# Softmax sums of an attention kernel: broadcast through DRAM in place of a TensorE transpose, halves added on GpSimd

## The chip, the cores and the metric

The kernel runs on one NeuronCore of a Trainium2 chip. The metric is the device time of one execution in microseconds (us). Before the change it is 2939.41 us, the median of three runs (2938.95 to 2943.35).

## What is computed

A backbone of two layers over 1024 latent tokens and 256 context tokens, width 1024: a Conformer convolution layer, then a grouped-query attention layer, each followed by a dense SwiGLU FFN. The change lies in the attention:

```python
def gqa_sdpa(q, k, v):
    B, Q, H, Dh = q.shape                      # 16 heads of 64, 4 key heads
    qg = q.reshape(B, Q, N_KV_HEADS, KV_GROUP, Dh)
    s = jnp.einsum("bqkgd,bskd->bkgqs", qg, k).astype(jnp.float32) * (Dh ** -0.5)
    p = jax.nn.softmax(s, axis=-1).astype(v.dtype)
    o = jnp.einsum("bkgqs,bskd->bqkgd", p, v)
    return o.reshape(B, Q, H * Dh)
```

In the second layer only the latent tokens ask: 1024 queries against 1280 keys.

## The kernel before

Everything is in fp32, and a product in full precision is built of fp32r products of high and low parts. The attention is cut into 32 units: one unit is one key head `t` with its 4 query heads and 128 queries (`attn_stream`). The scores of a unit (`scores`, L1116) are 24 matmuls, which fill two PSUM regions of 128x1280 in turn. VectorE scales a region into SBUF and takes its minimum (L1122), ScalarE does the exponential with the row sum as a side result (L1124). Then `values` works on the unit, while the scores of the next unit run: for each of 10 key tiles, TensorE transposes the probabilities of four heads (L1134), ScalarE rounds the tile to its high part (L1137), VectorE subtracts it for the low part (L1138), and two matmuls with the values add to the accumulator `av` (L1140 high, L1141 low). The `av` accumulator is one PSUM bank (bank 7), so the next unit's first L1140 waits until the last reader of this unit has left it.

`av` holds, for each half of its 128 rows, a product with the high and one with the low part of the values. The end of a unit adds the halves (ScalarE copies one, L1151; VectorE adds the other, L1152), and divides by the softmax sums. The sums lie with the queries on partitions and are needed with the queries along the free axis: GpSimd repeats the reciprocals (L1147), TensorE transposes them into the same bank 7 (L1155), and VectorE multiplies (L1156). The result goes to DRAM (`od`, issued by GpSimd, L1450); the last unit of a half stays in SBUF (`olast`).

Units 0 to 15 (the first 512 queries) run first. During units 0 and 1, projections of the layer run beside them; units 2 to 15 have the engines to themselves (called the attention stage here, 1641.6 to 1848 us). Units 16 to 31 run beside the output projection and the FFN of the first half (1848 to about 2395 us; 1995 to 2350 is called the FFN stage). The order of each engine's queue is made when the kernel is built, by a scheduler that takes the program's order, priorities (`later`) and its own estimate of durations. GpSimd's queue also issues the loads of queries (`load_q`, L1102: two slots, so a load waits until the unit before has finished its scores) and of keys (`load_k`, L1095: two buffers for units 0 to 15, one afterwards). SBUF scratch `sb` is a ring of four tiles.

Of the kernel before, what the change touches and what calls it, by code (L numbers as in the profile page):

```python
# [8 lines left out]
F32 = mybir.dt.float32  # L9
# [3 lines left out]
ALU = mybir.AluOpType  # L13
AX = mybir.AxisListType

P = 128
# [4 lines left out]
TOK = CTX + SEQ  # L21
# [3 lines left out]
NH, NKV, HD = 16, 4, 64  # L25
# [30 lines left out]
class Kern:  # L56
# [1071 lines left out]
    def values(self, t, Ps, sums, dst, done):  # L1128
        nc, c = self.nc, self.c
        av = self.bank("av")  # L1130
        for j in range(NJ):
            tp = self.bank("pt")
            for h in range(4):
                nc.tensor.transpose(tp[:, h * P:(h + 1) * P], Ps[h][:, j * P:(j + 1) * P], c["ident"])  # L1134
            ph, pl = self.ptring[self.ptslot % len(self.ptring)]
            self.ptslot += 1
            nc.scalar.copy(ph, tp)  # L1137
            nc.vector.tensor_tensor(pl, tp, ph.bitcast(F32), op=ALU.subtract)  # L1138
            with self.later(self.lav):
                nc.tensor.matmul(av, lhsT=self.value(t, j), rhs=ph, start=j == 0, stop=False)  # L1140
                nc.tensor.matmul(av, lhsT=self.value(t, j), rhs=pl, start=False, stop=j == NJ - 1)  # L1141
            yield 0.87

        r = sums[:, 1, :]
        nc.vector.reciprocal(r, sums[:, 0, :])
        rx = self.sb(256)
        nc.gpsimd.tensor_copy(rx.rearrange("p (h d) -> p h d", d=HD), r.unsqueeze(2).to_broadcast([P, 4, HD]))  # L1147
        tmp = self.sb(256).rearrange("p (a q) -> p a q", q=P)
        v = av.rearrange("p (a b q) -> p a b q", b=2, q=P)
        for b, r, o in ((0, slice(0, 64), slice(64, 128)), (1, slice(64, 128), slice(0, 64))):  # L1150
            nc.scalar.copy(tmp[r], v[o, :, b, :])  # L1151
            nc.vector.tensor_tensor(dst[r], v[r, :, b, :], tmp[r], op=ALU.add)  # L1152
        rb = self.bank("av")
        for a in range(2):
            nc.tensor.transpose(rb[:, a * P:(a + 1) * P], rx[:, a * P:(a + 1) * P], c["ident"])  # L1155
        nc.vector.tensor_tensor(dst, dst, rb[:, 0:256].rearrange("p (a q) -> p a q", q=P), op=ALU.mult)  # L1156
        done()
        yield 0.1

# [270 lines left out]
    def attention(self, final, qr):  # L1430
        nc, a, c = self.nc, self.a, self.c
        kbuf = self.T("T3", [P, 2 * TOK], F32R)
        pr1 = self.T("T1", [P, 3, TOK])
        prh = self.T("HS", [P, 4, TOK])
        ptt = self.T("T2", [P, 4, 2, 512], F32R)
        self.ptring = [(ptt[:, i, 0], ptt[:, i, 1]) for i in range(4)]
# [6 lines left out]
        def dst(q0):  # L1443
            def of(t, q):
                if (t, q % 4) == (NKV - 1, 3):
                    return self.olast, lambda: None
                st = self.sb(256).rearrange("p (a q) -> p a q", q=P)

                def done():
                    nc.gpsimd.dma_start(self.od[:, 2 * t:2 * t + 2, q * P:(q + 1) * P], st)  # L1450
                return st, done
            return of
# [11 lines left out]
        pr4 = None  # L1464
        for us in self.attn_stream(units, (self.kub, kbuf), dst(0), True):
            if self.bgq:
                self.pump(self.rate * us)
            elif pr4 is None:
                pr4 = self.T("T5", [P, 3, TOK])
                self.pring = self.pring[:4] + [pr4[:, 0], pr4[:, 1], pr4[:, 2]] + self.pring[4:]  # L1470
                self.set_banks(**alone)
                self.sring = [0, TOK]
# [78 lines left out]
        yacc, n = self.acc(CTX), CTX  # L1551
# [172 lines left out]
```

## Time and profile before

| | |
|---|---|
| median of 3 runs | 2939.41 us |
| the profiled execution | 2938.98 us |
| its span, first to last instruction | 2937.2 us |
| TensorE matmul / weight load busy | 97% / 83% of the span |
| VectorE, ScalarE, GpSimd busy | 74%, 45%, 8% |
| share of TensorE in the chain that ended last | 86% |

The busy share of TensorE is modelled from pipelined matmuls, so it says that the engine had something in flight, not that it worked at its peak. The shares are means over stages that differ; the section on rows has them by stage.

### The profile page before, as it was taken

How to read it: one execution, taken by the hardware profiler on the slowest of the kernel's cores; microseconds unless marked ns; L12 is line 12 of the kernel's file. 1: busy time of each engine (PE TensorE's matmuls, PEld its weight loads, DVE VectorE, ACT ScalarE, POOL GpSimd, SP SyncE). 2: the span in 40 equal slices, each digit the busy share in tenths (PEclk: the TensorE clock that was granted, in tenths of full speed). 3: DMA queues.
4: the chain of work that ended last, by engine and by line, in shares of the span. 5: the costliest groups of instructions: out<-in, count | busy, mean ns of one | idle time of the engine just before them, and what ended most of it. 6: DMA issues, size and time to landing. Idle time of an engine off the chain costs nothing.

```text
span 2937.2 us, 42731 instructions
## 1 busy us (share of the span) xinstructions
PE 2847.7 (97%) x16462; PEld 2446.1 (83%) x16462; DVE 2160.7 (74%) x3746; ACT 1335.5 (45%) x2229; POOL 222.6 (8%) x377
## 2 busy tenths in 40 slices
PE   7999989999999999999999999989999999999998
PEld 6888877888888889989888787767777778889997
DVE  6887788847556378877786899786666666786777
ACT  5222255532222245544445688645555543444444
POOL 0000001011022001000011111110000000010000
PEclk9999999999999999999999999999999999999999
DMA  6443444334356224333345211322222143353332
GB/s 249 140 120 98 116 131 145 135 116 143 115 175 198 65 74 165 114 104 112 109 156 170 88 46 46 97 87 81 66 73 83 60 149 99 110 170 104 102 98 75
DMA packets 131755, 336.58 MB, mean 115 GB/s; under 512 B 31328, under 2 KB 52864, under 8 KB 130656
## 3 DMA queue, kind: packets, MB, share of 16 engines
q1 hardware_dynamic: 78016, 222.33, 24.1%
q0 software_dynamic: 29344, 103.83, 10.7%
q10 hardware_dynamic: 24192, 7.70, 1.1%
q8 instruction: 129, 2.11, 0.3%
q14 instruction: 74, 0.61, 0.1%
HBM read 289.50 MB, written 38.93 MB: 112 GB/s over the span
## 4 chain that ended last, share of the span: by engine, by line
PE 86%; DVE 7%; ACT 2%; issue 2%; DMA 2%; ACTq 0%; POOL 0%; SPq 0%; DVEq 0%; POOLq 0%
PE ps L172 15%; PE ps L173 15%; PE ps L174 15%; PE ps L875 4%; PE ps L877 4%; PE ps L876 4%; PE ps L1116 4%; PE ps L1134 4%; PE ps L1140 2%; PE ps L454 2%; PE ps L455 2%; PE ps L456 2%; PE ps L1141 2%; PE ps L185 1%; PE ps L183 1%
## 5 line engine op out<-in xcount | busy, mean ns | idle before, releaser
L172 PE MATMUL ps<-T,wh 128*128 128x512 f32 (+1 forms) x1360 | 502.5, 370 | 1.4 <-ACT T L161 0.8
L174 PE MATMUL ps<-T,wl 128*128 128x512 f32 (+1 forms) x1360 | 500.4, 368 | 2.0 <-DVE wl L148 2.0
L173 PE MATMUL ps<-T,wh 128*128 128x512 f32 (+1 forms) x1312 | 481.4, 367 | 0.2 <-DVE T L164 0.2
L144 ACT CAST wh<-wr 128x1024 fp32r<-128x1024 f32 (+1 forms) x217 | 225.0, 1037 | 419.9 <-PE ps L173 307.2
L148 DVE TENSOR_TENSOR wl<-wr,wh 128x1024 fp32r<-128x1024 f32 (+1 forms) x217 | 261.9, 1207 | 168.5 <-ACT wh L144 167.1
L875 PE MATMUL ps<-T,wh 128*128 128x256 f32 x1092 | 310.7, 285 | 5.0 <-ACT wh L161 4.5
L876 PE MATMUL ps<-T,wh 128*128 128x256 f32 x1092 | 306.5, 281 | 0.0
L877 PE MATMUL ps<-T,wl 128*128 128x256 f32 x1092 | 305.4, 281 | 0.2 <-DVE wl L164 0.2
L1138 DVE TENSOR_TENSOR T<-ps,T 128x512 fp32r<-128x512 f32 x320 | 216.8, 687 | 107.6 <-ACT T L1137 106.8
L172 PEld LDWEIGHTS ps<-T,wh 128*128 128x128 f32 x1360 | 257.8, 190 | 43.7 <-ACT T L1506 1.7
L174 PEld LDWEIGHTS ps<-T,wl 128*128 128x128 f32 x1360 | 257.7, 190 | 42.4 <-DVE wl L148 2.2
L173 PEld LDWEIGHTS ps<-T,wh 128*128 128x128 f32 x1312 | 248.5, 189 | 38.2 <-DVE T L164 1.3
L1137 ACT CAST T<-ps 128x512 fp32r<-128x512 f32 x320 | 186.0, 586 | 191.1 <-PE ps L1134 177.6
L173 PE MATMUL ps<-HS,wh 128*128 128x512 f32 x656 | 257.9, 393 | 0.0
L172 PE MATMUL ps<-HS,wh 128*128 128x512 f32 x608 | 238.4, 392 | 0.9 <-ACT wh L144 0.9
L174 PE MATMUL ps<-HS,wl 128*128 128x512 f32 x608 | 237.5, 391 | 0.0
L875 PEld LDWEIGHTS ps<-T,wh 128*128 128x128 f32 x1092 | 206.1, 189 | 11.2 <-ACT wh L161 6.7
L876 PEld LDWEIGHTS ps<-T,wh 128*128 128x128 f32 x1092 | 206.6, 189 | 0.5
L877 PEld LDWEIGHTS ps<-T,wl 128*128 128x128 f32 x1092 | 206.2, 189 | 0.6 <-DVE wl L164 0.4
L1134 PE MATMUL ps<-cst,T 128*128 128x128 f32 x1100 | 189.6, 275 | 3.2 <-DVE T L1138 3.1
L1122 DVE TENSOR_SCALAR_CACHE_REDUCE T<-ps,rq 128x1280 f32<-128x1280 f32 x110 | 170.0, 1546 | 27.9 <-PE ps L1116 22.1
L1134 PEld LDWEIGHTS ps<-cst,T 128*128 128x128 f32 x1100 | 132.6, 141 | 49.5 <-DVE T L1138 30.8
(377 smaller groups left out, 6195.9 us busy)
## 6 DMA issues: line engine op xcount, KB each, us to landing
wr<-in_w SPq DMA_DIRECT2D x170, 512.0 KB, 3.6
wr<-in_pw SPq DMA_DIRECT2D x35, 512.0 KB, 3.5
HV<-in_wmodT POOLq DMA_DIRECT2D x56, 256.0 KB, 4.1
q<-in_wmodT POOLq DMA_DIRECT2D x56, 256.0 KB, 3.9
KB<-in_w SPq DMA_DIRECT2D x24, 512.0 KB, 3.6
HR<-in_w SPq DMA_DIRECT2D x23, 512.0 KB, 3.7
q<-in_w SPq DMA_DIRECT2D x23, 512.0 KB, 4.2
q<-qsd POOLq DMA_DIRECT2D x32, 256.0 KB, 3.3
```

The source lines that it names most:

```text
L144: nc.scalar.copy(hi, raw)
L148: nc.vector.tensor_tensor(lo, raw, hi.bitcast(F32), op=ALU.subtract)
L172: nc.tensor.matmul(out[:, :n], lhsT=wh, rhs=xh, start=k == 0, stop=False)
L173: nc.tensor.matmul(out[:, :n], lhsT=wh, rhs=xl, start=False, stop=False)
L174: nc.tensor.matmul(out[:, :n], lhsT=wl, rhs=xh, start=False, stop=k == nk - 1)
L875: nc.tensor.matmul(out, lhsT=wh, rhs=bh, start=first and k == 0, stop=False, **skip)
L876: nc.tensor.matmul(out, lhsT=wh, rhs=bl, start=False, stop=False, **skip)
L877: nc.tensor.matmul(out, lhsT=wl, rhs=bh, start=False, stop=k == 3, **skip)
L1122: nc.vector.tensor_scalar(out=pt, in0=sc, scalar1=rq[:, h:h + 1], scalar2=None, op0=ALU.mult, op1=ALU.min, accum_out=mn)
L1134: nc.tensor.transpose(tp[:, h * P:(h + 1) * P], Ps[h][:, j * P:(j + 1) * P], c["ident"])
L1137: nc.scalar.copy(ph, tp)
L1138: nc.vector.tensor_tensor(pl, tp, ph.bitcast(F32), op=ALU.subtract)
```

## The change

The reciprocals are taken at the beginning of `values` rather than at the end. GpSimd writes them to a DRAM scratch (`rsd`) with heads and queries swapped, 512 elements of 4 bytes, and reads them back twice, each time broadcast over 64 partitions, into a buffer `rb`. There is one `rb` behind the probability rows in T1, and a second one behind those in T5 as soon as T5 is there. At the end of a unit ScalarE copies both halves (four copies), and GpSimd adds and multiplies. The repeat on GpSimd, the two transposes, and VectorE's two adds and one multiply are gone.

```diff
     def values(self, t, Ps, sums, dst, done):
         nc, c = self.nc, self.c
         av = self.bank("av")
+        r = sums[:, 1, :]
+        nc.vector.reciprocal(r, sums[:, 0, :])
+        rd = self.rsd[self.unit]
+        rb = self.rbs[self.unit % len(self.rbs)]
+        self.unit += 1
+        nc.gpsimd.dma_start(rd.rearrange("h q -> q h"), r)
+        rv = rd.rearrange("(a b) q -> b a q", b=2)
+        for b in range(2):
+            nc.gpsimd.dma_start(rb[b * HD:(b + 1) * HD], rv[b:b + 1].to_broadcast([HD, 2, P]))
         for j in range(NJ):
...
-        r = sums[:, 1, :]
-        nc.vector.reciprocal(r, sums[:, 0, :])
-        rx = self.sb(256)
-        nc.gpsimd.tensor_copy(rx.rearrange("p (h d) -> p h d", d=HD), r.unsqueeze(2).to_broadcast([P, 4, HD]))
         tmp = self.sb(256).rearrange("p (a q) -> p a q", q=P)
         v = av.rearrange("p (a b q) -> p a b q", b=2, q=P)
         for b, r, o in ((0, slice(0, 64), slice(64, 128)), (1, slice(64, 128), slice(0, 64))):
             nc.scalar.copy(tmp[r], v[o, :, b, :])
-            nc.vector.tensor_tensor(dst[r], v[r, :, b, :], tmp[r], op=ALU.add)
-        rb = self.bank("av")
-        for a in range(2):
-            nc.tensor.transpose(rb[:, a * P:(a + 1) * P], rx[:, a * P:(a + 1) * P], c["ident"])
-        nc.vector.tensor_tensor(dst, dst, rb[:, 0:256].rearrange("p (a q) -> p a q", q=P), op=ALU.mult)
+            nc.scalar.copy(dst[r], v[r, :, b, :])
+        nc.gpsimd.tensor_tensor(dst, dst, tmp, op=ALU.add)
+        nc.gpsimd.tensor_tensor(dst, dst, rb, op=ALU.mult)
         done()
@@ def attention
-        pr1 = self.T("T1", [P, 3, TOK])
+        def place(tag):
+            t = self.T(tag, [P, 3 * TOK + 2 * P])
+            return t[:, :3 * TOK].rearrange("p (i n) -> p i n", i=3), t[:, 3 * TOK:].rearrange("p (a q) -> p a q", q=P)
+        pr1, rb = place("T1")
+        self.rbs, self.unit = [rb], 0
+        self.rsd = self.dp.tile([2 * NKV * 4, 4, P], F32, tag="rsd", name="rsd")
...
-                pr4 = self.T("T5", [P, 3, TOK])
+                pr4, rb = place("T5")
+                self.rbs.append(rb)
```

In the changed kernel the lines move: L1134 becomes L1143, L1137 L1146, L1138 L1147, L1140 L1149, L1141 L1150, L1151 L1156 with L1157 new beside it, L1450 L1458; L1136 is the write to `rsd`, L1139 the reads, L1158 and L1159 the add and the multiply. The scheduler lays the queues anew.

TensorE's queue at the end of a unit in the attention stage, before (L1116 scores, L1134 transposes of probabilities, L1155 the transposes of reciprocals, L1140 the first matmul of the next unit into bank 7):

```order
L1116 MATMUL ps<-KB,q 128x512 x2
L1134 MATMUL ps<-cst,T_13569 128x128
L1134 MATMUL ps<-cst,T_14068 128x128 x3
L1116 MATMUL ps<-KB,q 128x256 x2
L1116 MATMUL ps<-KB,q 128x512
L1155 MATMUL ps<-cst,sb 128x128 x2
L1116 MATMUL ps<-KB,q 128x512 x2
L1134 MATMUL ps<-cst,T_13569 128x128
L1134 MATMUL ps<-cst,T_14068 128x128 x2
L1140 MATMUL ps<-T_13571,HV 128x512
```

And in the changed kernel, from the last matmul of a unit (L1150) to the first of the next (L1149):

```order
L1150 MATMUL ps<-T_13572,HR 128x512
L1143 MATMUL ps<-cst,T_13569 128x128
L1143 MATMUL ps<-cst,T_14073 128x128 x3
L1116 MATMUL ps<-KB,q 128x512 x3
L1116 MATMUL ps<-KB,q 128x256 x2
L1149 MATMUL ps<-T_13572,HV 128x512
L1150 MATMUL ps<-T_13572,HV 128x512
L1143 MATMUL ps<-cst,T_13569 128x128
```

The next unit's first L1149 now stands behind one tile of transposes and five score matmuls; the pair L1155 is gone.

ScalarE's queue around the same place, before (L1151 the copies, L1137 the rounding of tiles, L1124 the exponentials):

```order
L1137 CAST T_13571<-ps 128x512 x6
L1151 COPY sb<-ps 64x256
L1124 ACTIVATE T_13569,sums<-T_13569,mn 128x1280
L1151 COPY sb<-ps 64x256
L1137 CAST T_13571<-ps 128x512 x2
L1124 ACTIVATE T_14068,sums<-T_14068,mn 128x1280
```

The same in the changed kernel:

```order
L1146 CAST T_13572<-ps 128x512 x5
L1124 ACTIVATE HS,sums<-HS,mn 128x1280
L1146 CAST T_13572<-ps 128x512
L1156 COPY sb<-ps 64x256
L1157 COPY sb<-ps 64x256
L1156 COPY sb<-ps 64x256
L1157 COPY sb<-ps 64x256
L1146 CAST T_13572<-ps 128x512
```

The four copies stand in a row, with no exponential between them.

GpSimd's queue at the first change of keys among units 16 to 31, before (L1095 the two halves of the keys):

```order
L1450 DMA od<-sb 128x2x128
L1095 DMA KB<-ksd 64x2560 x2
L1450 DMA od<-sb 128x2x128
L1102 DMA q<-qsd 128x4x128
L1147 COPY sb<-sums 128x256
```

The same in the changed kernel:

```order
L1136 DMA rsd<-sums 128x4x1
L1139 DMA T_13569<-rsd 64x2x128 x2
L1158 TENSOR_TENSOR sb<-sb 128x256
L1159 TENSOR_TENSOR sb<-sb,T_14073 128x256
L1458 DMA od<-sb 128x2x128
L1095 DMA KB<-ksd 64x2560
L1158 TENSOR_TENSOR sb<-sb 128x256
L1095 DMA KB<-ksd 64x2560
L1159 TENSOR_TENSOR sb<-sb,T_13569 128x256
L1102 DMA q<-qsd 128x4x128
L1458 DMA od<-sb 128x2x128
```

The second half of the keys now stands behind an add that waits for ScalarE's copies; at the two later changes of keys the halves stay together.

## Rows read from the trace of the kernel before

**Rows 1.** Busy time by stage, the first column from:to in us.
```profile
core 0: us, PE busy (x) PEld busy (x) DVE busy (x) ACT busy (x) POOL busy (x), PEclk, DMA share, GB/s
1641.60:1848.00 206.40, 198.57 (x1192) 161.66 (x1191) 187.41 (x308) 166.85 (x280) 29.66 (x48) 1.00 0.17 47
1995.00:2350.00 355.00, 354.96 (x1833) 279.65 (x1831) 235.35 (x346) 194.47 (x303) 26.09 (x41) 1.00 0.25 73
```
**Rows 2.** Chain that ended last, by line, 1641.6 to 1848.
```profile
by line: PE ps L1134 19.9%; PE ps L1116 18.2%; PE ps L1140 13.9%; PE ps L1141 12.9%; DVE T L1138 9.7%; issue 6.9%; DVE T L1122 6.0%; ACT T L1137 4.2%; DVE HS L1122 3.9%; DVE sb L1152 2.2%; PE ps L1155 1.5%; ACT sb L1151 0.5%; ACT T L1124 0.
```
**Rows 3.** Chain that ended last, by line, 1995 to 2350.
```profile
by line: PE ps L172 17.0%; PE ps L174 17.0%; PE ps L173 16.9%; PE ps L1116 16.1%; PE ps L1134 15.5%; PE ps L1140 8.3%; PE ps L1141 8.1%; PE ps L1155 1.1%; issue 0.0%
```
**Rows 4.** Groups, 1641.6 to 1848: busy us, mean ns | idle before, releaser.
```profile
L1152 DVE TENSOR_TENSOR sb<-ps,sb 64x256 f32<-64x256 f32 x28 | 11.7, 417 | 0.4
L1151 ACT COPY sb<-ps 64x256 f32<-64x256 f32 x28 | 10.3, 368 | 0.7
L1156 DVE TENSOR_TENSOR sb<-sb,ps 128x256 f32<-128x256 f32 x14 | 5.7, 410 | 0.0
L1147 POOL COPY sb<-sums 128x256 f32<-128x256 f32 x14 | 5.6, 400 | 22.9 <-DVE sums L1145 10.1 <-issue 7.1 <-DMA od<-sb 5.1
L1102 POOL DMA_DIRECT2D q<-qsd x14 | 10.8, 770 | 90.6 <-PE ps L1116 85.5 <-PE ps L1134 5.1
L1450 POOL DMA_DIRECT2D od<-sb x14 | 10.1, 721 | 61.5 <-DVE sb L1156 60.2 <-issue 1.2
L1095 POOL DMA_DIRECT2D KB<-ksd x4 | 2.2, 540 | 0.0
```
**Rows 5.** Timeline of one handover of bank 7 in the attention stage.
```profile
1704.96 0.37 ACT L1151 COPY sb<-ps 64x256 f32<-64x256 f32 x1
1705.50 0.41 DVE L1152 TENSOR_TENSOR sb<-ps,sb 64x256 f32<-64x256 f32 x1
1706.43 1.53 DVE L1122 TENSOR_SCALAR_CACHE_REDUCE HS<-ps,rq 128x1280 f32<-128x1280 f32 x1
1708.02 0.73 PE L1116 MATMUL ps<-T,q 128*128 128x256 f32 x3 [0.56 <-DVE HS L1122]
1709.07 0.41 DVE L1156 TENSOR_TENSOR sb<-sb,ps 128x256 f32<-128x256 f32 x1
1709.54 0.49 PE L1140 MATMUL ps<-T,HV 128*128 128x512 f32 x1
```
**Rows 6.** Timeline of TensorE without gaps: 512, 256 and 128 columns.
```profile
1710.67 0.40 PE L1140 MATMUL ps<-T,HR 128*128 128x512 f32 x1
1710.90 0.39 PE L1141 MATMUL ps<-T,HR 128*128 128x512 f32 x1
1715.25 0.28 PE L1116 MATMUL ps<-T,q 128*128 128x256 f32 x1
1715.37 0.40 PE L1141 MATMUL ps<-T,HR 128*128 128x512 f32 x1
1716.07 0.27 PE L1134 MATMUL ps<-cst,T 128*128 128x128 f32 x1
1716.18 0.27 PE L1134 MATMUL ps<-cst,HS 128*128 128x128 f32 x1
```
**Rows 7.** DMA issues of the whole span: KB each, median us to landing.
```profile
od<-sb POOLq DMA_DIRECT2D x30, 128.0 KB, 2.6
q<-qsd POOLq DMA_DIRECT2D x32, 256.0 KB, 3.3
KB<-ksd POOLq DMA_DIRECT2D x10, 640.0 KB, 7.1
T<-in_wmod SPq DMA_DIRECT2D x12, 512.0 KB, 10.5
KB<-HR SPq DMA_DIRECT2D x40, 16.0 KB, 1.9
```
**Rows 8.** L1147 alone, whole span: duration ns min/median/max.
```profile
L1147 POOL COPY sb<-sums x32: 394/402/1365, 1605.4 to 2363.0; 128x256 f32<-128x256 f32 x32
```
**Rows 9.** Timeline of GpSimd at three places, of VectorE at the second.
```profile
1650.10 0.77 POOL L1102 DMA_DIRECT2D q<-qsd  x1 [1.36 <-PE ps L1116]
1671.35 1.54 DVE L1122 TENSOR_SCALAR_CACHE_REDUCE HS<-ps,rq 128x1280 f32<-128x1280 f32 x1
2008.39 1.07 POOL L1095 DMA_DIRECT2D KB<-ksd  x2 [19.04 <-PE ps L1116]
2013.58 0.74 POOL L1450 DMA_DIRECT2D od<-sb  x1 [4.12 <-DVE sb L1156]
```
**Rows 10.** Chain in order of time: the scores behind the new keys.
```profile
2018.24 1.17 PE ps L1116 x6
```

## The prediction

> **What bounds the kernel now.** I read the busy time by stage first. In the attention stage (units 2 to 15) three engines are nearly full: of 206.4 us VectorE is busy 187.41 (91%), ScalarE 166.85 (81%), TensorE 198.57 by its modelled ends [rows 1]. In the FFN stage TensorE is busy 354.96 of 355.00 and VectorE 235.35 [rows 1]. Then the chain of waits by line. In the attention stage VectorE's lines L1138, L1122 and L1152 hold 21.8% of it, with 6.9% issue [rows 2]; in the FFN stage nothing but TensorE is in it, and issue is 0.0% [rows 3]. So VectorE's time is worth something in the first place and nothing in the second, where only TensorE's own instructions count.
>
> How much is there to win in the attention stage? A unit takes 206.4 / 14 = 14.74 us. TensorE's spacing without gaps is 0.23 us for 512 columns (1710.67 to 1710.90), 0.12 for 256 (1715.25 to 1715.37) and 0.11 for a 128-column transpose [rows 6]. A unit's 24 score matmuls are 8 sets of 512 + 512 + 256 columns, 8 x 0.58 = 4.64; its 40 transposes 40 x 0.11 = 4.40; its 20 value matmuls 4.60; the two L1155 0.22. That is 13.86 with L1155 and 13.64 without; 0.88 us of a unit TensorE waits. One such wait is in the timeline: L1152 pushes the following VectorE work, L1122 frees a score region only at 1707.96, and TensorE's L1116 starts at 1708.02 after 0.56 idle [rows 5].
>
> **The change part by part.**
>
> *VectorE.* Two L1152 of 417 ns and one L1156 of 410 ns leave each unit: 1.24 us [rows 4]. The reciprocal is only moved. VectorE's 187.41 / 14 = 13.39 us per unit becomes 12.15.
>
> *ScalarE.* Two more copies of 368 ns [rows 4]: 0.74 us, from 166.85 / 14 = 11.92 to 12.66 per unit. The four stand together and wait for the unit's last value matmul, in front of the next tiles and exponentials. In the order they come behind a tile's transposes, and TensorE has another tile and five score matmuls in front of the next unit's first value matmul: 0.44 + 3 x 0.23 + 2 x 0.12 = 1.37 us, against 4 x 0.37 = 1.48 us of copies. So bank 7 is handed over with almost no gap; before it took from 1704.96 to 1709.54, 4.6 us, through both engines and TensorE [rows 5].
>
> *TensorE.* 0.22 us of transposes per unit by spacing [rows 6]; the chain of the FFN stage gives 1.1% of 355 us for the 12 units in it, 0.33 us each [rows 3].
>
> *The attention stage.* The floor is now TensorE's 13.64; VectorE (12.15) and ScalarE (12.66) lie under it, but close enough that two score regions and two transpose banks will not hide every delay. The two bounds are 13.64, no wait left, and 14.52, all waits left and only L1155 gone. I take the middle of the old wait, 13.64 + 0.41 = 14.05: a gain of 0.69 x 14 = 9.7 us (bounds 3.1 and 15.4).
>
> *Units 16 to 31.* TensorE is the bound, so 16 x 0.22 to 16 x 0.33 = 3.5 to 5.3 us; I take 4.0. What VectorE and ScalarE save or pay there is covered by TensorE's FFN matmuls (VectorE 235 of 355, ScalarE 194 of 355 [rows 1]).
>
> *GpSimd.* No row shows a two-input operation on GpSimd. The copy of the same size takes 0.40 us, and 1.365 at the longest [rows 8]; I take 0.80, twice the copy, and keep both ends. The write of 4-byte pieces is in no row either: landings go from 1.9 to 10.5 us [rows 7]; I take 2.6, that of `od`, which has the same queue and direction. GpSimd's queue holds for a unit: query load 0.77, write 0.77 (priced as the query load, which also has 512 pieces), two reads 2 x 0.54 (as one half of the keys), `od` 0.72 [rows 4], add and multiply 1.6, and the wait for the landing 2.6: 7.5 us of 14.05. The multiply's own data come a unit early, since write and reads are issued at the beginning of a unit's values. `od` lands later than it did by at most some microseconds, and its tile is one of four, asked for again two units on. So I cost it at nothing in the attention stage. If the cover goes, ScalarE's copies wait for a free `sb` tile, and everything in ScalarE's queue with them.
>
> The Trainium skill speaks against the move itself: "GPSIMD Engine Reference", section 4.1 (Engine selection), wants elementwise work with two inputs on VectorE, as GpSimd takes about twice as long, and section 3.1 gives about 2.6 cycles per element at 1.2 GHz, by which 256 elements would take an estimated 0.56 us; the pair would be 1.1 us, and GpSimd's sum 7.0. No run here shows it yet, and by either price GpSimd keeps half of the unit free.
>
> *What the queue is moved past.* Query loads now stand behind add, multiply and `od`: the load issued at 1650.10 lands 3.3 us later [rows 7, 9], and its unit's first L1122 is at 1671.35 [rows 9], so 18 us are free. An ISA instruction in front of the first add falls under the same cover; its time is in no row. Key loads have less. At the first change of keys in units 16 to 31 both halves were issued by 2009.5 and take 7.1 us, to 2016.6, and the first scores start at 2018.24 [rows 7, 9, 10]: 1.6 us are free. The second half now waits for an add that waits for ScalarE's copies. The old `od`, which followed the same accumulator's end, was issued at 2013.58 [rows 9], so the half might go out 2 to 4 us late: 0 to 3 us on TensorE, once. I take 1.
>
> *Sum.* The profiled execution took 2938.98 us (span 2937.2 and 1.8 around it), 0.4 below the median, so I work from it: 2938.98 - 9.7 - 4.0 + 1.0 = 2926.3 us.
>
> **The rivals.**
>
> *A, the forecast:* VectorE relieved, TensorE the bound: 2926.3. Its own range is 2938.98 - 15.4 - 5.3 = 2918 to 2938.98 - 3.1 - 3.5 + 3 = 2935.
>
> *B, ScalarE takes VectorE's place:* the four copies wait for the last value matmul, and the exponentials and tiles behind them wait too. ScalarE has 14.74 - 12.66 = 2.1 us free in a unit; if the copies idle it that long, the attention stage keeps 14.74 and only units 16 to 31 gain, less 0.5 for the keys: 2938.98 - 4.0 + 0.5 = 2935.5. For it: tiles already wait for each other along TensorE, ScalarE and VectorE in turn. Against: no idle before L1151 worth naming, 0.7 us over 28 copies [rows 4], and the order gives the bank a cover of 1.37 us.
>
> *C, slower: GpSimd's round trip is the bound of the attention stage.* The read waits in GpSimd's queue until the write has landed, and add, multiply, `od` and query load stand behind it. With the longest landing, 10.5 us [rows 7], the queue needs 7.5 + 7.9 = 15.4 us per unit: 0.66 x 14 = 9.2 us more in the attention stage, less 4.0 in units 16 to 31, where TensorE has the time: 2938.98 + 9.2 - 4.0 + 1.0 = 2945. It decides from a landing of 9.9 us (14.74 - 4.9 of other work). For it: 512 pieces of 4 bytes. Against: 16 KB land in 1.9 us, and the 10.5 belong to 512 KB [rows 7]. The skill's "DMA: Bandwidth & Descriptors", in its rules for kernel authors, says that a last dimension that is not contiguous becomes one descriptor per element and should be rearranged, which is this write's form; no row shows such a write.
>
> **How the numbers follow.** A has 0.68, B 0.17, C 0.10, and 0.05 is left for orders of the queues that none of these describes. A measurement of this kernel can tell 0.2%, 5.9 us, from no change. A up to 2933 is faster: 0.66, and 0.04 of the rest with B's better end makes 0.70. The upper end of A and most of B are within 0.2%: 0.18. C and a part of the rest are slower: 0.12. The range goes from A's low end, 2917.5, up past B to 2940, and leaves out C.
>
> **What would show it.** Right: 1641.6 to the end of unit 15 shrinks from 206 to about 197 us; VectorE's share there falls from 91% to about 87%, and its lines lose most of their 21.8% in the chain; the first value matmul of a unit starts under 2 us after the last of the unit before; in the FFN stage TensorE stays the whole chain. B: idle time before the copies on ScalarE, released by TensorE, near 2 us per unit. C: L1139 waits near 10 us for `rsd`, and L1156 waits for GpSimd or `od`. A wrong sign would come from TensorE idle in the FFN stage that was not there before, at L1116 behind late keys or queries above all.

## The result, and the profile after

The changed kernel takes 2951.4 us (median of 6 runs, 2949.28 to 2957.13), the kernel before 2940.7 beside it (6 runs): ratio 1.0042, 95% interval 1.0032 to 1.0052. It is 0.4% slower where 0.4% faster was forecast. The profiled execution took 2957.13 us (span 2955.3), the slowest of the six.

Where it went is read best from the start of each TensorE instruction against the same instruction in the kernel before. In this execution 5 us stand there already at 1600 us, before any changed code runs; that is scatter between executions. Counted from there, in us (where the order of the queues differs from the kernel before, single instructions scatter, and a value is good to 1 or 2 us):

```
time in the kernel before     1600   1820   1900   1940   2340   2500
changed kernel                   0   +2.3   +9.9  +11.7  +13.3  +12.8
forecast                         0   -9     -9.7   -9.7  -12    -12.7
```

So the attention stage, which was to give 9.7 us, lost 2. The transition behind it, where no term stood, lost 7.6. The FFN stage, which was to give 4, lost 3.

Busy time by stage, columns as in [rows 1], with the transition between them:

```profile
core 0: us, PE busy (x) PEld busy (x) DVE busy (x) ACT busy (x) POOL busy (x), PEclk, DMA share, GB/s
1641.60:1848.00 206.40, 197.51 (x1134) 157.31 (x1134) 172.19 (x266) 170.76 (x301) 70.13 (x101) 0.98 0.27 59
1848.00:1995.00 147.00, 128.77 (x603) 100.31 (x602) 107.02 (x180) 80.95 (x132) 28.65 (x42) 0.92 0.37 92
1995.00:2350.00 355.00, 351.68 (x1800) 277.93 (x1799) 220.12 (x308) 203.47 (x330) 61.67 (x90) 1.00 0.38 78
```

VectorE fell from 91% to 83% of the attention stage, as the change promised, and yet the stage is no shorter. One unit takes 14.84 us from reciprocal to reciprocal (1718.7 to 1837.4 for eight) against 14.70 before (1741.5 to 1829.7 for six). What TensorE waits for in those eight units (engine, what waits, releaser: us in total, times, longest), the kernel before first, eight units too (1712.1 to 1829.7), its matmuls (PE) and its weight loads (PEld):

```profile
PE ps L1116 <- DVE HS L1122: 2.3, 4, 0.6
PE ps L1116 <- DVE T L1122: 0.8, 4, 0.2
PEld ps L1134 <- DVE T L1138: 3.4, 16, 0.2
PEld ps L1116 <- DVE T L1122: 3.3, 8, 0.5
PEld ps L1116 <- DVE HS L1122: 3.2, 4, 0.8
```

and the changed kernel:

```profile
PE ps L1149 <- ACT sb L1157: 4.2, 8, 0.5
PEld ps L1149 <- ACT sb L1157: 5.8, 8, 0.7
PEld ps L1143 <- DVE T L1147: 4.6, 16, 0.3
PEld ps L1116 <- DVE T L1122: 1.9, 8, 0.3
```

The waits for VectorE's L1122 are gone from the matmuls and fell from 6.5 us to 1.9 at the weight loads, and in every unit a wait of 0.52 us stands in front of L1149, the first value matmul (L1140 before). Its releaser is L1157, the last of ScalarE's four copies. The handover of bank 7 that answers to [rows 5]:

```profile
1754.63 0.48 PE L1150 MATMUL ps<-T,HR 128*128 128x512 f32 x1
1754.91 0.58 ACT L1146 CAST T<-ps 128x512 fp32r<-128x512 f32 x1
1755.31 1.25 PE L1116 MATMUL ps<-KB,q 128*128 128x512 f32 x5
1755.52 0.37 ACT L1156 COPY sb<-ps 64x256 f32<-64x256 f32 x1
1755.90 0.36 ACT L1157 COPY sb<-ps 64x256 f32<-64x256 f32 x1
1756.28 0.36 ACT L1156 COPY sb<-ps 64x256 f32<-64x256 f32 x1
1756.65 0.37 ACT L1157 COPY sb<-ps 64x256 f32<-64x256 f32 x1
1757.07 0.50 PE L1149 MATMUL ps<-T,HV 128*128 128x512 f32 x1 [0.52 <-ACT sb L1157]
```

From the first copy to the first value matmul the handover fell from 4.6 us to 1.6 (1755.52 to 1757.07). The four copies last 1.5 us, as forecast, and TensorE's cover ends at 1756.55, 0.52 before L1149. But the copies begin only at 1755.52, 0.4 us after the value matmul they wait for has ended (1755.11): a tile's cast (L1146, 0.58 us) stands in front of them in ScalarE's queue. No run moves that cast; its part is read from this timeline.

GpSimd's timeline over one unit:

```profile
1793.39 0.77 POOL L1136 DMA_DIRECT2D rsd<-sums  x1 [0.73 <-DVE sums L1132]
1794.15 0.55 POOL L1095 DMA_DIRECT2D KB<-ksd  x1
1803.57 1.20 POOL L1139 DMA_DIRECT2D T<-rsd  x2 [8.88 <-DMA rsd<-sums]
1804.78 0.76 POOL L1158 TENSOR_TENSOR sb<-sb 128x256 f32<-128x256 f32 x1
1805.62 0.74 POOL L1159 TENSOR_TENSOR sb<-sb,T 128x256 f32<-128x256 f32 x1
1806.65 0.75 POOL L1458 DMA_DIRECT2D od<-sb  x1 [0.29 <-POOL sb L1159]
1807.40 0.77 POOL L1102 DMA_DIRECT2D q<-qsd  x1
1808.20 0.75 POOL L1136 DMA_DIRECT2D rsd<-sums  x1
```

and over the whole span the landings of L1136's write, then of L1139's reads:

```profile
DMA to landing us min/median/max: 7.8/9.9/12.3
...
DMA to landing us min/median/max: 2.6/3.4/6.4
```

The write lands after 9.9 us (the prediction took 2.6), and GpSimd's round from write to write is 14.8 us, as long as the unit. This is a unit with key loads (L1095); over the stage GpSimd has slack in front of the write, 12.1 us for VectorE's reciprocals:

```profile
L1136 POOL DMA_DIRECT2D rsd<-sums x14 | 10.6, 760 | 12.7 <-DVE sums L1132 12.1 <-DVE T L1147 0.6
```

The chain of the stage, which answers to [rows 2], puts this first:

```profile
by line: DMA rsd<-sums 22.8%; PE ps L1143 16.4%; PE ps L1116 14.3%; PE ps L1149 9.9%; PE ps L1150 7.6%; issue 5.9%; ACT sb L1157 3.2%; ACT T L1146 2.9%; DMA KB<-ksd 2.8%; ACT sb L1156 2.7%; POOL T L1139 2.1%; ACT T L1124 1.9%; POOL q L1102 
```

The experiments show that in this stage the chain misleads. In the transition it doesn't. The chain in order of time (start us, us, what), and what waited there:

```profile
1852.69 0.75 POOL rsd L1136
1853.43 1.75 issue
1855.19 12.16 DMA HS<-od
...
1867.90 0.59 ACT T L1146
...
1868.54 0.80 PE ps L1149
```
```profile
ACT T L161 <- DMA HS<-od: 7.6, 1, 7.6
...
PE ps L1149 <- ACT T L1146: 6.8, 1, 6.8
```

The output projection's first load (`HS<-od`) is issued 2.5 us behind unit 15's write in the same GpSimd queue and lands 12.16 us later. ScalarE's L161, which rounds the loaded tile to its high part, waits 7.6 us for it, the tile's cast L1146 stands behind L161, and TensorE waits 6.8 us. That is nearly the whole step of 7.6 in the table. The load wasn't issued late: 1855.19 is 1848.28 of the kernel before plus the 7 us by which this execution lies behind there, and there it landed after 4.2 us. Behind the wait TensorE's granted clock also falls, to 0.66 as the mean of 10 us (in part its lower level, 1.2 GHz), where the kernel before kept 1.00 at the same place (the columns of the first table):

```profile
1865.00:1875.00 10.00, 6.46 (x26) 5.04 (x26) 6.30 (x11) 6.38 (x12) 2.96 (x5) 0.66 0.62 179
```
```profile
1860.00:1870.00 10.00, 8.82 (x45) 6.97 (x43) 8.63 (x14) 6.47 (x10) 2.44 (x4) 1.00 0.38 122
```

### The profile page after: what moved, and what is told of

Read it like the earlier page. It is cut to its first block, busy times and chain, and to the rows that moved or that the text cites. A ratio compares the mean times of both kernels' runs of the same rounds, so it can differ in the third digit from the quotient of the medians.

```text
span 2955.3 us, 42686 instructions
## 1 busy us (share of the span) xinstructions
PE 2855.5 (97%) x16398; PEld 2450.1 (83%) x16398; DVE 2127.5 (72%) x3650; ACT 1356.1 (46%) x2293; POOL 320.0 (11%) x505
## 4 chain that ended last, share of the span: by engine, by line
PE 55%; DVE 4%; DMA 3%; ACT 3%; issue 2%; POOL 1%; ACTq 0%; DVEq 0%; POOLq 0%
PE ps L172 9%; PE ps L173 9%; PE ps L174 9%; PE ps L875 4%; PE ps L877 4%; PE ps L876 4%; PE ps L1143 4%; PE ps L1116 3%; DMA rsd<-sums 2%; PE ps L1149 2%; PE ps L1150 2%; PE ps L185 1%; PE ps L184 1%; PE ps L183 1%; ACT T L1124 1%
## 5 line engine op out<-in xcount | busy, mean ns | idle before, releaser
L1147 DVE TENSOR_TENSOR T<-ps,T 128x512 fp32r<-128x512 f32 x320 | 217.0, 687 | 135.9 <-ACT T L1146 135.4
L1146 ACT CAST T<-ps 128x512 fp32r<-128x512 f32 x320 | 186.2, 585 | 187.6 <-PE ps L1143 179.5
L1143 PE MATMUL ps<-cst,T 128*128 128x128 f32 x1100 | 192.7, 278 | 6.1 <-DVE T L1147 3.9
L1122 DVE TENSOR_SCALAR_CACHE_REDUCE T<-ps,rq 128x1280 f32<-128x1280 f32 x110 | 170.2, 1547 | 34.3 <-PE ps L1116 30.2
L1143 PEld LDWEIGHTS ps<-cst,T 128*128 128x128 f32 x1100 | 134.7, 142 | 56.9 <-DVE T L1147 31.8
```

The source lines that it names most:

```text
L1122: nc.vector.tensor_scalar(out=pt, in0=sc, scalar1=rq[:, h:h + 1], scalar2=None, op0=ALU.mult, op1=ALU.min, accum_out=mn)
```

## The experiments

All ratios are to the kernel before run beside them, with 95% intervals; its median stands with each group. Every edit also lets the scheduler lay the queues anew, so a run shows its edit together with the order that comes with it. In the table, offsets as above, counted from 1600 us:

```
                         median   ratio [95%]              unit   1820   1900   1940   2500
one write                2943.7  1.0014 [1.0006, 1.0023]  14.82   +2.3   +2.5   +4.2   +5.3
SyncE's queue            2953.3  1.0045 [1.0033, 1.0058]  14.82   +1.9   +8.0   +9.7  +15.5
DRAM alone               2949.3  1.0033 [1.0021, 1.0045]  15.02   +2.9  +12.5  +13.5  +10.0
transposed in pt bank    3026.6  1.0295 [1.0282, 1.0309]  16.80
two copies               2936.5  0.9985 [0.9976, 0.9994]  14.2    -7.2   +0.2   +0.6   -2.7
two copies, one write    2927.3  0.9954 [0.9941, 0.9968]  14.2    -7.0   -7.0   -6.4  -12.2
short rows               2945.1  1.0013 [1.0005, 1.0022]  14.87   +2.6   +3.2   +5.0   +4.7
wide copy                2930.1  0.9966 [0.9953, 0.9978]         -10.4   -8.9   -4.3   -7.3
wide copy early          2926.4  0.9953 [0.9941, 0.9966]         -10.9   -9.2   -6.8  -12.4
reciprocal early         2942.5  1.0007 [0.9998, 1.0016]  15.02   +1.9   +1.8   +2.5   +2.8
```

**First group** (before: 2939.3 us). *One write*, against the changed kernel:

```diff
-        rd = self.rsd[self.unit]
+        rd = self.rsd[0]
...
-        nc.gpsimd.dma_start(rd.rearrange("h q -> q h"), r)
+        if self.unit == 1:
+            nc.gpsimd.dma_start(rd.rearrange("h q -> q h"), r)
```

> The changed kernel, but the 4-byte write of the reciprocals is made for the first unit alone, and the reads of all units take its row; the sums of the other 31 units are left out of the result. Reads, add, multiply and the four ScalarE copies stay. Theory W (GpSimd stands behind the landing of that write, median 9.9 us, in every unit): L1139 stops waiting, GpSimd's round of 14.8 us per unit falls to about 5 to 7, the attention stage goes from 206 to 194-200 us, the 6.8 us idle of TensorE near 1868 goes with it, and the time is 2928 to 2936 us, below the kernel before (2940.7). Rival S (the four ScalarE copies hold bank 7 and delay the tiles behind them): the attention stage keeps its 206 us or more and the time stays at 2947 to 2952 us. Rival M (both): 2938 to 2945 us.

2943.7 us: 8 us less than the changed kernel by the ratios (0.0028 x 2940), but still above the kernel before. The unit keeps 14.82 us, with TensorE's wait in front of the first value matmul unchanged (4.2 us in eight units). What goes is the transition's step: from 1820 to 1900 the offset moves by 0.2 instead of 7.6. So W holds for the transition alone, and of the expectations only M, "both", came out.

*SyncE's queue*: `nc.gpsimd.dma_start` becomes `nc.sync.dma_start` for the write and the two reads.

> The changed kernel with the write and the two reads of the reciprocals issued by SyncE instead of GpSimd; the landing itself is as before. Theory W, in its form that the wait in GpSimd's queue is the cost: add, multiply, output and query load no longer stand behind the landing; the multiply's data come about 10 + 3.4 us after the write, within a unit of 14 us, so the attention stage falls below 206 us, to about 198-202, and the time to 2930-2938 us. If it is the landing as such, wherever it is awaited (the reads come too late for the multiply): 2945 to 2952 us. Rival S: 2947 to 2952 us.

2953.3 us, no better. The landing is still 9.2 us (median), the transition loses 6.1 us, and at the first change of keys it loses 5 more. W in its form "the wait in GpSimd's queue" is refuted. The wait for the landing now stands in SyncE's queue, and keys come late (SyncE from 1600 to 2100 us last, TensorE between 2015 and 2045 first):

```profile
PE ps L1116 <- DMA KB<-ksd: 3.3, 1, 3.3
```
```profile
SPq L1139 <- DMA rsd<-sums: 189.7, 22, 12.6
```

This run shows one thing more. The write went out in SyncE's queue at 1845.88, and three loads of the output projection in GpSimd's, from 1848.65 on. Their landings, in the kernel before first:

```profile
DMA to landing us min/median/max: 4.2/5.3/5.9
```
```profile
DMA to landing us min/median/max: 10.1/10.7/12.7
```

So what is in flight beside the 4-byte write lands late though it stands in another queue. Why isn't shown.

*DRAM alone*:

```diff
-            nc.scalar.copy(dst[r], v[r, :, b, :])
-        nc.gpsimd.tensor_tensor(dst, dst, tmp, op=ALU.add)
-        nc.gpsimd.tensor_tensor(dst, dst, rb, op=ALU.mult)
+            nc.vector.tensor_tensor(dst[r], v[r, :, b, :], tmp[r], op=ALU.add)
+        nc.vector.tensor_tensor(dst, dst, rb, op=ALU.mult)
```

> One part alone: reciprocals through DRAM on GpSimd's queue, but add and multiply stay on VectorE, and ScalarE makes its two copies as before the change. Theory W: GpSimd's queue still waits about 10 us per unit, but now only query loads and outputs stand behind it and the unit's last multiply is VectorE's, which would wait for the reads in its own queue: if these land in time the kernel is within 0.2% of the one before, 2936 to 2943 us; if they don't, VectorE stands still and everything with it, over 2950 us. Rival S (the ScalarE copies cost): the loss is gone, 2934 to 2938 us, since TensorE's 0.22 us per unit are saved and nothing is added to ScalarE.

2949.3 us, inside neither theory's numbers. The transition loses 9.6 us here too; the output projection's first load, issued 2.7 us behind a write, lands after 10.9 us. The unit rose to 15.02 us, though nothing but the reciprocal's place was added to VectorE; the last run takes that up.

*Transposed in a transpose bank*:

```diff
-        nc.gpsimd.dma_start(rd.rearrange("h q -> q h"), r)
...
+        nc.gpsimd.tensor_copy(rx.rearrange("p (h d) -> p h d", d=HD), r.unsqueeze(2).to_broadcast([P, 4, HD]))
+        rp = self.bank("pt")
+        for a in range(2):
+            nc.tensor.transpose(rp[:, a * P:(a + 1) * P], rx[:, a * P:(a + 1) * P], c["ident"])
+        nc.vector.tensor_copy(rb, rp[:, 0:256].rearrange("p (a q) -> p a q", q=P))
```

> The other part alone: no DRAM; the reciprocals are transposed on TensorE at the beginning of a unit's values, into a transpose bank, and copied to SBUF by VectorE; the four ScalarE copies, and add and multiply on GpSimd, stay as in the changed kernel. Theory W: GpSimd's queue never waits for a landing; VectorE loses 1.24 us per unit and gains a copy of about 0.4: the attention stage falls to about 199-203 us, TensorE keeps its 0.22 us per unit: 2932 to 2939 us, below the kernel before. Rival S: 2945 to 2955 us, as in the changed kernel.

3026.6 us: a failed experiment. It adds a cost of its own, so it tells the two theories nothing. The broadcast takes one of the transpose banks until VectorE has copied it out, and the tiles' transposes (L1145 here) wait through the whole stage, 12.4 us in seven units against 4.6 in eight of the changed kernel. TensorE's weight loads in 1721.8 to 1839.4:

```profile
PEld ps L1145 <- DVE T L1149: 12.4, 35, 0.6
```

Its loss of some 50 us after the attention stage was not followed up.

**Second group** (before: 2940.1 us). The wait of 0.52 us in front of the first value matmul was now the suspect. *Two copies* takes two of the four away, with the landing (*two copies*) and without it (*two copies, one write*), so that with the changed kernel and *one write* there are four corners:

```diff
-            nc.scalar.copy(dst[r], v[r, :, b, :])
-        nc.gpsimd.tensor_tensor(dst, dst, tmp, op=ALU.add)
+        nc.gpsimd.tensor_tensor(dst, tmp, tmp, op=ALU.add)
```

> The changed kernel with two ScalarE copies per unit instead of four; the straight half of the accumulator is left out of the result (the add takes the crossed half twice). DRAM write, landing, GpSimd's add and multiply stay. Theory H (in the attention stage the four copies in a row hold bank 7, TensorE waits 0.5 us in front of the first value matmul of every unit, and that is why the stage gained nothing): the period falls from 14.84 us per unit toward 14.3, and the time by some 7 us, to 2942-2946 us. Theory G (GpSimd's round of 14.8 us with the landing in it is the bound of the stage too): the period stays at 14.8, the time within 2 us of the changed kernel, 2948-2952 us.

> The same two copies instead of four, and the 4-byte write made for the first unit alone, as in the run with one write (both the straight half and the sums of the other units are left out of the result). Theory H: period 14.3 us, 7 to 8 us less than with one write alone (2943.7): 2934-2938 us. If neither the landing nor the copies set the period (order, or TensorE's own work): 14.8 us and 2941-2945 us. With the run before this gives the two causes apart and together.

```
ratio               write in every unit   one write   difference
four copies               1.0042            1.0014      8 us
two copies                0.9985            0.9954      9 us
difference                 17 us             18 us
```

Two causes, additive within the intervals (4 to 5 us either way for each difference): the two extra copies cost 17 us, twice what H expected, so that both times lie below its range, and the landing 8 to 9. The unit falls to 14.2 us with the landing as long as ever (9.4 us median), so G, GpSimd's round as the bound of the stage, is refuted: a round without key loads is 13.3 us there (1794.63 to 1807.95), and the chain's 22.8% bound nothing in the stage. About 9 of the copies' 17 us are the attention stage; 6 to 8 are the FFN stage. There the copies stand in ScalarE's queue in front of exponentials and casts, and TensorE waits for those. *One write* (1890 to 2380):

```profile
PE ps L1144 <- ACT T L1124: 2.4, 7, 0.4
...
PEld ps L1144 <- ACT T L1124: 6.4, 11, 0.8
PEld ps L1150 <- ACT T L1147: 10.8, 42, 0.9
```

*Two copies, one write* (1884 to 2370), where the matmuls no longer wait for L1124 (their waits for other casts, 1.4 and 1.6 us, are the same):

```profile
PEld ps L1144 <- ACT T L1124: 2.4, 9, 0.5
PEld ps L1150 <- ACT T L1147: 7.5, 26, 0.9
```

These rows account for a part of the 6 to 8 us; the order of TensorE's queue differs between the two, and the rest wasn't followed.

*Short rows* changes the form of the write alone:

```diff
-        nc.vector.reciprocal(r, sums[:, 0, :])
+        nc.vector.reciprocal(rp[:, 0:4], sums[:, 0, :])
+        nc.vector.transpose(rt, rp)
...
-        nc.gpsimd.dma_start(rd.rearrange("h q -> q h"), r)
+        nc.gpsimd.dma_start(rd, rt)
...
+            for k in range(2):
+                nc.gpsimd.dma_start(rb[b * HD:(b + 1) * HD, k].rearrange("p (j q) -> p j q", j=4),
+                                    rv[b:b + 1, k].to_broadcast([HD, 4, 32]))
...
```

> Whole result. The reciprocals are turned by VectorE in 32x32 blocks and written as 128 pieces of 128 bytes instead of 512 of 4; the broadcast is then read in four DMAs instead of two (1.2 us more of GpSimd's issue). Theory W (the loss in the transition comes from the landing of the 4-byte write, 7.7 us by the run with one write): the landing falls to 2-4 us, the transition's loss goes, the attention stage keeps 14.8 us per unit: 2942-2947 us. If small writes land late whatever their form: landing 8-10 us and 2949-2955 us.

2945.1 us, as W expected, and the landing of its write:

```profile
DMA to landing us min/median/max: 1.7/1.7/7.2
```

512 pieces of 4 bytes land in 9.9 us; eight times the bytes, in 128 pieces of 128, land in 1.7. The transition's step is gone and the attention stage stays, as with *one write*.

*Wide copy* adds to this one copy of the whole bank, so that ScalarE releases it with one instruction:

```diff
+        w = self.sb(512)
+        nc.scalar.copy(w, av)
+        v = w.rearrange("p (a b q) -> p a b q", b=2, q=P)
...
-            nc.scalar.copy(tmp[r], v[o, :, b, :])
-            nc.scalar.copy(dst[r], v[r, :, b, :])
-        nc.gpsimd.tensor_tensor(dst, dst, tmp, op=ALU.add)
+            nc.gpsimd.tensor_copy(tmp[r], v[o, :, b, :])
+            nc.gpsimd.tensor_tensor(dst[r], v[r, :, b, :], tmp[r], op=ALU.add)
```

> Whole result, a version that might beat both: 128-byte pieces as in the run with short rows, and ScalarE releases bank 7 with one copy of 128x512 (0.59 us as the copies of the tiles) instead of four of 0.37; GpSimd crosses the halves, adds and multiplies from SBUF (two copies and one add more, about 1.5 us). Theory H and W together: period 14.3 us or less, no loss in the transition: 2930-2938 us, below the kernel before (2939.3). If GpSimd's queue becomes long (over 14 us per unit): 2945 us or more.

2930.1 us, 10 us below the kernel before. The one copy (1718.7 to 1837.4) costs 0.6 us where four cost 1.47:

```profile
L1158 ACT COPY sb<-ps 128x512 f32<-128x512 f32 x8 | 4.8, 595 | 0.0
```

The stage gives 10.4 us. From 1820 to 1940, 6 are lost again, most of it from 1900 on.

**Third group** (before: 2940.9 us). *Wide copy early* keeps it for the first 15 units and gives the rest ScalarE's two copies and VectorE's adds and multiply as in the kernel before, with the scale from DRAM:

```diff
+        cross, sums2 = (nc.gpsimd.tensor_copy, nc.gpsimd) if wide else (nc.scalar.copy, nc.vector)
...
+            cross(tmp[r], v[o, :, b, :])
+            sums2.tensor_tensor(dst[r], v[r, :, b, :], tmp[r], op=ALU.add)
+        sums2.tensor_tensor(dst, dst, rb, op=ALU.mult)
```

> Whole result. As the version with the wide copy for the first 15 units; from unit 15 on (the transition and the FFN stage) the kernel before's arrangement: two ScalarE copies, VectorE adds from the bank and multiplies, with the scale still from DRAM in 128-byte pieces. Theory (VectorE's relief is worth something only in the attention stage; after it GpSimd's 3 us chain of two copies, two adds and one multiply delays the transition, where the version with the wide copy lost about 5 us, and gains nothing in the FFN stage): 2922-2928 us, 2 to 8 us below that version (2930). If the FFN stage wants VectorE free as well: 2930-2936 us.

2926.4 us, 14 below the kernel before and the lowest of those that compute the whole result; the interval overlaps that of the wide copy. In the attention stage (1712 to 1812) no matmul of TensorE waits, and no weight load waits more than 0.3 us, as here behind the wide copy:

```profile
PEld ps L1152 <- ACT sb L1160: 1.2, 4, 0.3
```

From 1940 on it gains 5.6 us where the wide copy gained 3. Between 1900 and 1940 it loses 2.4 where the wide copy lost 4.6; GpSimd's longer work explains at most that difference. The 1.5 to 2 us lost from 1820 to 1900 are the same in both, and their traces show a wait there: ScalarE's L161 again waits for `HS<-od` (2.9 and 3.2 us), TensorE waits 3.4 us for casts (1.2 in the kernel before), and its granted clock falls (0.50 from 1855 to 1860 with the wide copy, 0.66 from 1850 to 1855 here; 1.00 in the kernel before). The rest stays open.

*Reciprocal early* moves the reciprocal, in the kernel before:

```diff
         av = self.bank("av")
+        r = sums[:, 1, :]
+        nc.vector.reciprocal(r, sums[:, 0, :])
...
-        nc.vector.reciprocal(r, sums[:, 0, :])
```

> The kernel before with one thing moved: VectorE's reciprocal stands at the beginning of a unit's values, as in the changed kernel; broadcast on TensorE, copies and adds are as before. If the move is free: period 14.70 us and 2938-2942 us. If the wait of the reciprocal for the last exponential (0.3 us per unit in the runs with DRAM) costs VectorE in the attention stage, where it is the bound: period 14.9-15.05 us (the DRAM-only run had 15.02) and 2943-2946 us.

The unit rises from 14.70 to 15.02 us, exactly that of *DRAM alone*, whose attention stage is explained by it: VectorE, the bound there, now waits in every unit for the last exponential. That is the pace of the later units; the offset at 1820 is +1.9 us. In the whole time it is 1.0007, an interval that takes in no change, just below the range expected for that case. VectorE from 1712 to 1829:

```profile
DVE sums L1132 <- ACT T L1124: 3.3, 7, 0.5
```

## Why the prediction was wrong, step by step

- **What bounds the stage: right.** With two of the copies gone a unit takes 14.2 us at the end of the stage (14.05 and 14.09 as means of units 4 to 14, by the starts of their first exponentials; 14.05 forecast, bounds 13.64 to 14.52), and the stage gives 7 to 11 us (9.7 forecast, bounds 3.1 to 15.4). VectorE's relief is what does it: *DRAM alone* and *two copies* differ in the adds and the multiply (VectorE or GpSimd) and in the half left out, and take 15.02 and 14.2. The middle of a wait of 0.88 is 0.44, not the 0.41 of the sum; that slip decides nothing.
- **VectorE: "The reciprocal is only moved"** put the move at nothing. Alone, in the kernel before, it takes a unit from 14.70 to 15.02 us. In the changed kernel VectorE isn't the bound, and what the move costs there isn't shown.
- **ScalarE: the first failed step**, "So bank 7 is handed over with almost no gap". Copies (1.48 us, measured 1.5) and TensorE's instructions in front were sized well. The cast that stands in front of the copies in ScalarE's own queue, 0.58 us, was left out of the sum; it holds them up by 0.4. So TensorE waited 0.52 us in every unit, and 2.4 us lay between the last value matmul and the next unit's first (1754.63 to 1757.07), where under 2 was to show the step right. The wait is 0.52 of the 0.79 us by which the unit exceeds its forecast; the two extra copies together are worth most of it (14.84 against 14.2). It isn't rival B as written: B's sign, ScalarE idle in front of the copies, is 0.3 us over 16 copies (the last figure of the row), and it is TensorE that waits. In the stage it used up the gain: +2.3 instead of -9.7.

```profile
L1156 ACT COPY sb<-ps 64x256 f32<-64x256 f32 x16 | 5.9, 366 | 0.3
```

- **Units 16 to 31: the same step again**, "What VectorE and ScalarE save or pay there is covered". ScalarE's 57% busy says nothing about order: the extra copies delay exponentials and casts that TensorE waits for. From 1900 to 2500 us two copies gave 5.2 us with one write and 2.9 with the landing (bounds 3.5 to 5.3); four lost 1.5 to 2.9. A sign named for a wrong outcome came true, TensorE idle in the FFN stage, but not behind keys or queries. Its matmuls from 1995 to 2350 us in the changed kernel; in the kernel before there is no such row:

```profile
PE ps L1143 <- DVE T L1147: 1.7, 5, 0.4
PE ps L1143 <- ACT T L1124: 1.6, 5, 0.4
```

- **GpSimd: the second failed step**, the landing "I take 2.6, that of `od`, which has the same queue and direction"; it is 9.9. The bounds went to 10.5, and the longer value was given to rival C alone. In the attention stage "I cost it at nothing" was right, even with the long landing. The add and the multiply take 0.73 to 0.75 us, near the 0.80 taken; VectorE's multiply of that size took 0.41 [rows 4]. So the Trainium skill's "GPSIMD Engine Reference", section 4.1, about twice as long, agrees with the trace; the estimate of 0.56 by its section 3.1 is too low here.
- **"What the queue is moved past" missed the place where it matters.** It priced keys and queries, where the changed kernel lost nothing (between 2000 and 2030 us the offset moves by 0.1, against the 1 us of the sum). The output projection's first load, at the transition, wasn't listed, and the sum had no term for what the write does to a transfer in flight beside it: 12.16 us to land instead of 4.2. It cost 7.6 us. *SyncE's queue* shows that the order in one queue isn't the cause, since loads of another queue came as late.
- **Rival C** came near in its time (2945) and in what it told to look for, L1139 waiting near 10 us. But its place was wrong: the round of 14.8 us in the attention stage wasn't the bound; the landing was paid once, at the transition. The rule that it cited from the Trainium skill's "DMA: Bandwidth & Descriptors", rules for kernel authors, that a last dimension that is not contiguous becomes one descriptor per element, agrees with the traces: over 500 packets of 4 bytes to a write in *SyncE's queue*, and 9.9 us against 1.7 for whole rows.
- **The sum.** Forecast -13 us, measured +12 (0.0042 x 2940): 25 us apart. The corners give 17 for the copies and 8 for the landing. That *two copies, one write* comes out at -13.5 is in part luck: it leaves out two copies that the forecast had in its sum.

## What to carry to other kernels

An engine's relief is worth what the next wait leaves of it: when accumulators are handed over, count everything that stands in front of the copies in their engine's queue, and release the bank with one wide instruction rather than four narrow ones. Before a small transfer is put in a queue, look at its pieces, not its bytes, and list every transfer that will be in flight beside it, in other queues too, at the stage's end above all. A share in the chain of waits is a suspicion; here 22.8% of it was worth nothing in its own stage, and only taking the wait away showed it.

## What the runs showed of the hardware

- A unit's reciprocals are 2 KB in 512 pieces of 4 bytes: 7.8 to 12.3 us to land. 16 KB in 128 pieces of 128 bytes: 1.7 us (median). A 512 KB load issued 2.5 us behind the first in GpSimd's queue landed after 12.16 us.
- Other queues feel it too. Three loads in GpSimd's queue landed after 10.1 to 12.7 us beside a write in SyncE's (4.2 to 5.9 in the kernel before). In the changed kernel, 13 of SyncE's 512 KB weight loads went out while such a write of GpSimd's was in flight: 9.9 us (median) to land, against 3.7 for the 29 that met none.
- ScalarE's copy out of PSUM takes 0.366 us for 64x256 and 0.595 for 128x512. If, as in the next line, the number of partitions doesn't count, the 256 columns more cost 0.229 us, and 0.137 of the short copy is fixed (an estimate from the two rows). Of the 0.87 us that one wide copy saves over four short ones, about half is then the fixed part and half the columns: the short ones pass 1024 columns on half the partitions, the wide one 512.
- GpSimd's two-input operation takes 0.73 us on 64x256 and 0.74 on 128x256: half the partitions take the same time.
